# A 32-expert mixture kernel: third expert matrix read by row halves, both output halves accumulated together, first gate weights split before the overflow loop

## The chip, the cores and the metric

The program runs on one core of one Trainium2 chip. The metric is the device time of one execution in microseconds (us); lower is better. Three runs of the kernel before gave 2838.57, 2838.99 and 2841.83 us, a median of 2838.99. The profile is of another execution, of 2839.78 us.

Engines are named as in the profile: PE is the matrix engine (PEld its weight loads), DVE the vector engine, ACT the scalar engine, POOL GpSimd, SP the engine that issues most transfers. L932 means line 932 of the kernel before.

## The reference

A sequence of 1024 tokens of width 1024 goes through a mixer block, a mixture of experts, a gated addition, and two hybrid layers. The change lies in the experts and in the gate. Cut to what matters, the computation there is:

```python
# hier_moe: every token goes to 2 of 32 experts; per expert e, x: its rows
y = (silu(x @ w1[e]) * (x @ w3[e])) @ w2[e]     # w1, w3: 1024x512, w2: 512x1024, fp32
h = h + weighted_sum_of_the_two_y
# gate
h = h + rms_norm(p @ w_ple, g_ple) * sigmoid(rms_norm(h, g_plg) @ w_plg)   # w_plg: 1024x1024
```

All of it is fp32. The kernel keeps that precision by splitting each fp32 operand into a high and a low part and by adding three products: high by high, high by low weights, low by high weights.

## The kernel before

**An expert.** `moe()` (L1019) loops over 32 experts; `expert()` (L917) is a generator that does one. A gathered tile of 128 tokens (`xg`) is transposed on PE (L942), copied high by ACT (`exh`, L924) and low by DVE (`exl`, L926). The six weight pieces of an expert are 1 MB each (128 partitions by 2048 values): w1.0, w1.1, w3.0, w3.1 are row halves of w1 and w3; w2.0 and w2.1 are column halves of w2, which means 2 KB in one run of memory. I write e.w1.0 for such a piece of expert e. w1 goes into one PSUM bank, w3 into another, each with 24 matmuls of 128x512 (two halves of four 128-row blocks, three matmuls a block, L932 to L934). ACT takes the silu (`esg`, L959, two instructions), DVE multiplies (`ehd`, L960, two instructions), PE transposes four times (L965), ACT and DVE split the result (`ehh`, `ehl`). Then w2: for one column half after the other, 12 matmuls into a PSUM bank of its own and an evacuation by ACT (`ey`, L974); at the end POOL scatters the 128 rows to memory (`y_d`, L975). 72 matmuls of 128x512 and 12 transposes make an expert.

**Splitting weights.** A landed piece is split in four blocks of 128x512: ACT writes the high part (L115), DVE subtracts it from the raw data to get the low part (L116). The order of pieces is fixed by `seq`: e.w1.1, e.w3.1, (e+1).w1.0, (e+1).w3.0, e.w2.0, e.w2.1. Every third split goes to a single buffer `mhi`/`mlo`: these are e.w1.1 and (e+1).w3.0, in turn. The other four go to the two `whi`/`wlo` buffers in turn: e.w3.1 and e.w2.0 use one of them, (e+1).w1.0 and e.w2.1 the other. A split can only overwrite a buffer when the matmuls of the piece that was in it are done. Raw data lands in seven buffers that are used in a circle; SP issues the next load when the low part of the piece in a buffer is done.

**Order.** Each engine runs its instructions in the order of one list. That order is not the order of the Python code: a scheduler builds it, with its own estimate of when operands are ready. So one expert's w2 is mixed with the next expert's w1 and w3, and a change of a few lines can reorder the whole stage. Experts 4 to 11 also carry a tile of another product, `ple` (L699 to L708).

**Overflow and gate.** After the experts comes a loop for tokens that did not fit (`overflow()`, L982), which has no rounds with these inputs; its branch is a point in each engine's list that instructions are not moved across. Then `plg()` (L1110) reads the scattered rows back (`res`, `cy`, L1131 and L1133), adds them up (L1148, L1152), transposes (L241), and multiplies with w_plg in `wide()` (L162). `wide` takes the tiles in groups of four; a group goes through the first half of the weight's rows, then the second. The weight halves are loaded (L124) and split with a scale: four ACT instructions (L141) and four DVE instructions (L142) each. `wide` also serves the output projections, where `prep` makes the left operand of a tile.

Of the kernel before, what the change touches and what calls it, by code (L numbers as in the profile page):

```python
# [10 lines left out]
AF = mybir.ActivationFunctionType  # L11
# [7 lines left out]
NT = SEQ // 128  # L19
# [27 lines left out]
class Kernel:  # L47
# [113 lines left out]

    def wide(self, a, src, evac, group=4, prep=None, g=None):  # L162

        nc = self.nc
        w = [None, None]
        for t0 in range(0, NT, group):
            ps = [self.mm_ps() for _ in range(group)]
            for hf in range(2):  # L170
                if t0 == 0:
                    w[hf] = self.load_w(src[hf * 512:hf * 512 + 512], 4, 512, g=None if g is None else g[:, hf * 4:hf * 4 + 4])
                wh, wl = w[hf]
                for j in range(group):
                    tt = t0 + j
                    if prep and hf == 0:
                        prep(tt)
                    ah, al = a[tt // 4]
                    sl = slice(tt % 4 * 128, tt % 4 * 128 + 128)
                    for k in range(4):  # L180
                        f, l, ka = hf + k == 0, hf + k == 4, hf * 4 + k
                        nc.tensor.matmul(ps[j], ah[:, ka, sl], wh[:, k], start=f, stop=False)  # L182
                        nc.tensor.matmul(ps[j], ah[:, ka, sl], wl[:, k], start=False, stop=False)  # L183
                        nc.tensor.matmul(ps[j], al[:, ka, sl], wh[:, k], start=False, stop=l)  # L184
                    if hf:
                        evac(ps[j], tt)
# [730 lines left out]
    def expert(self, wp, xg, w1, w3, w2, sidx, native, after=None):  # L917


        nc = self.nc  # L920
        dt = F32 if native else F32R
# [45 lines left out]
        yield  # L967
        y = wp.tile([128, D], F32, name="ey", bufs=1)
        for c in range(2):
            ww = w2(c)  # L970
            q = self.mm_ps()
            for k in range(4):
                mm(q, (hh, hl), k, ww[:, k] if native else (ww[0][:, k], ww[1][:, k]), k == 0, k == 3)
            nc.scalar.activation(y[:, c * 512:c * 512 + 512], q, AF.Copy)  # L974
        yield nc.gpsimd.indirect_dma_start(  # L975
# [8 lines left out]
    def overflow(self):  # L984
# [9 lines left out]
        with self.banks(tp=3, mm=5), self.pool(name="ov", bufs=1) as wp:  # L994
            with tc.For_i(0, n, 1) as b:
# [8 lines left out]
                def w(name, rows):  # L1004
                    def f(c):
                        t = wp.tile([128, 4, 512], F32, name="ow")
                        cs = slice(c * 512, c * 512 + 512)
                        src = I[name][0, bass.ds(e, 1)]
                        src = src[:, cs] if rows else src[:, :, cs]
                        nc.sync.dma_start(t, src.rearrange("o (k p) n -> p (o k) n", p=128))  # L1010
                        return t
                    return f

                list(self.expert(wp, xg, w("w1", True), w("w3", True), w("w2", False), ix[:, 1:2], True))
        pre = nc.scalar.activation(self.done, self.done, AF.Copy)
# [3 lines left out]
    def moe(self, pgp):  # L1019
# [9 lines left out]
        with self.pool(name="mraw", bufs=1) as rw, ExitStack() as xs:  # L1029
# [6 lines left out]
            def fetch(key):  # L1036
# [4 lines left out]
                raw = b[0].tile([128, 2048], F32, name="mraw", tag=b[1]) if b else self.w_raw()  # L1041
                cs = slice(c * 512, c * 512 + 512)
                raws[key] = self.load_raw(raw, I[nm][0, e][:, cs] if nm == "w2" else I[nm][0, e][cs], 4, 512, dma=MOE_DMA)

# [64 lines left out]
    def plg(self, res, ple, norm):  # L1109
# [7 lines left out]
        with self.pool(name="pgn", bufs=1, side="right") as np_:  # L1117
# [6 lines left out]
            for tt, h in enumerate(hs):  # L1124
                nc.sync.dma_start(h, self.h1_d[tt * 128:tt * 128 + 128])
            pre = self.overflow()

# [31 lines left out]
        with ph, self.pool(name="ln", bufs=1, side="right") as ln, self.pool(name="pgc", bufs=1) as cp:  # L1159
# [4 lines left out]
            for c in range(2):  # L1164
# [12 lines left out]

                self.wide(ga, I["w_plg"][0][:, cs], evac, g=g)
            self.begin(0, lambda: cp.tile([128, 512], F32, name="psg", bufs=2)[:, :256])
# [452 lines left out]
```

## Time and profile before

| what | value |
|---|---|
| median of three runs | 2838.99 us |
| profiled execution | 2839.78 us, span 2838.0 us |
| mean granted PE clock | 0.981 of full speed |
| expert stage | 817 to 1440 us |
| PE busy over the span | 2667.1 us, 94% |
| DVE busy | 2089.5 us, 74% |
| ACT busy | 1763.0 us, 62% |
| memory traffic by DMA | 512.19 MB |

The span is the profiled execution from its first to its last instruction; 1.8 us of the execution lie outside it. A busy PE is no sign of a PE at its limit, because the ends of matmuls are modelled; so the distance between two starts is read, not the duration of one. In the answers a row gives the start in us, the duration (of a group of several, from the first start to the last end), the engine, the line, the operation, and the tiles as output<-inputs; in brackets stands how long the engine was idle before and what released it. The time of the stage can be read from POOL's scatters, one for each expert.

### The profile page before, as it was taken

The numbers are of one execution on the slowest core, as the hardware profiler recorded it, in microseconds if no ns is written. First come the engines' busy times: TensorE is split into PE (matmuls) and PEld (weight loads), VectorE is DVE, ScalarE is ACT, GpSimd is POOL, SyncE is SP. The second block draws the span as 40 slices with busy tenths as digits, with TensorE's granted clock in tenths as the row PEclk, the third lists the DMA queues.
The fourth block names the chain that finished last, engine by engine and source line by source line (L and its number), as shares of the span: only waits on it lengthen the run. The fifth ranks groups of instructions, "written<-read, shape, count | busy, mean of one in ns | idle before, by whom it ended". The sixth has DMA issues, their size and how long they took to land.

```text
span 2838.0 us, 46020 instructions
## 1 busy us (share of the span) xinstructions
PE 2667.1 (94%) x16247; PEld 2345.2 (83%) x16247; DVE 2089.5 (74%) x4266; ACT 1763.0 (62%) x3828; POOL 659.5 (23%) x688
## 2 busy tenths in 40 slices
PE   7999989899989999999979899999999999999988
PEld 7998968798768777877768788899878889999866
DVE  6778679885489888999966478899355479898254
ACT  4444467784348878888866367788343378787242
POOL 0344041360001102111014102650124103630132
PEclk9999989999989999999989899999999999999999
DMA  7765532244469989999962332332563433332561
GB/s 234 252 215 171 147 106 68 52 85 150 164 233 345 320 312 354 367 362 366 366 250 90 116 115 89 100 97 69 206 218 104 132 112 99 90 97 85 213 193 75
DMA packets 382701, 512.19 MB, mean 180 GB/s; under 512 B 95973, under 2 KB 220925, under 8 KB 381957
## 3 DMA queue, kind: packets, MB, share of 16 engines
q1 hardware_dynamic: 368068, 479.85, 51.2%
q0 software_dynamic: 14400, 29.38, 3.1%
q8 instruction: 129, 2.11, 0.3%
q14 instruction: 104, 0.84, 0.1%
HBM read 425.19 MB, written 101.97 MB: 186 GB/s over the span
## 4 chain that ended last, share of the span: by engine, by line
PE 25%; DVE 12%; ACT 5%; DMA 4%; issue 3%; POOL 1%; SPq 0%; DVEq 0%; ACTq 0%; POOLq 0%
PE mm L1278 3%; PE mm L1279 3%; PE mm L1280 3%; DVE sw L1452 3%; PE mm L184 2%; PE mm L183 2%; PE mm L182 2%; DMA sqk<-sk_d 2%; PE mm L158 2%; PE mm L160 2%; PE mm L159 2%; DVE sw L1451 1%; DVE sal L1471 1%; DVE sw L1457 1%; PE tp L1467 1%
## 5 line engine op out<-in xcount | busy, mean ns | idle before, releaser
L158 PE MATMUL mm<-whi,acth 128*128 128x256 f32 x1792 | 517.9, 289 | 11.3 <-DVE hn L325 3.4
L160 PE MATMUL mm<-whi,actl 128*128 128x256 f32 x1792 | 514.4, 287 | 0.2 <-DVE rsx L102 0.2
L159 PE MATMUL mm<-wlo,acth 128*128 128x256 f32 x1792 | 512.3, 286 | 0.0
L158 PEld LDWEIGHTS mm<-whi,acth 128*128 128x128 f32 x1792 | 345.1, 193 | 19.9 <-ACT rx L1319 4.8
L116 DVE TENSOR_TENSOR wlo<-mraw,whi 128x512 fp32r<-128x512 f32 x508 | 315.9, 682 | 48.1 <-ACT whi L115 47.8
L160 PEld LDWEIGHTS mm<-whi,actl 128*128 128x128 f32 x1792 | 344.5, 192 | 3.2 <-issue 0.7
L159 PEld LDWEIGHTS mm<-wlo,acth 128*128 128x128 f32 x1792 | 344.8, 192 | 2.6 <-issue 0.5
L115 ACT ACTIVATE whi<-mraw 128x512 fp32r<-128x512 f32 x508 | 276.0, 628 | 13.8 <-PE mm L934 8.6
L116 DVE TENSOR_TENSOR wlo<-wraw,whi 128x2048 fp32r<-128x2048 f32 (+1 forms) x60 | 132.9, 2219 | 126.0 <-ACT whi L115 123.9
L184 PE MATMUL mm<-whi,actl 128*128 128x512 f32 x512 | 202.0, 395 | 5.0 <-DVE actl L116 5.0
L182 PE MATMUL mm<-whi,acth 128*128 128x512 f32 x512 | 200.8, 397 | 4.7 <-ACT acth L115 4.7
L183 PE MATMUL mm<-wlo,acth 128*128 128x512 f32 x512 | 200.9, 393 | 1.4 <-DVE wlo L116 1.4
L1278 PE MATMUL mm<-acth,whi 128*128 128x512 f32 x512 | 201.4, 393 | 0.0
L1280 PE MATMUL mm<-acth,wlo 128*128 128x512 f32 x512 | 200.9, 392 | 0.0
L1279 PE MATMUL mm<-actl,whi 128*128 128x512 f32 x512 | 200.8, 392 | 0.0
L115 ACT ACTIVATE whi<-wraw 128x2048 fp32r<-128x2048 f32 (+1 forms) x60 | 109.4, 1827 | 97.9 <-PE mm L184 49.8
L116 DVE TENSOR_TENSOR mlo<-mraw,mhi 128x512 fp32r<-128x512 f32 x256 | 160.1, 680 | 2.9 <-ACT mhi L115 1.6
L1322 POOL TENSOR_TENSOR cN<-rx,rcos 128x256 f32<-128x256 f32 x64 | 58.6, 915 | 411.5 <-ACT rx L1319 407.8
L1458 ACT ACTIVATE sw<-sw 128x128 f32<-128x128 f32 (+2 forms) x192 | 100.1, 526 | 76.8 <-DVE sw L1457 75.6
L115 ACT ACTIVATE mhi<-mraw 128x512 fp32r<-128x512 f32 x256 | 140.6, 631 | 2.9 <-PE mm L934 2.9
L1451 DVE SCALAR_TENSOR_TENSOR sw<-z,sw 128x128 f32<-128x128 f32 (+1 forms) x192 | 103.8, 546 | 33.0 <-ACT sw L1450 32.4
L975 POOL DMA_INDIRECT y_d<-ey,sidx x32 | 38.9, 1216 | 372.2 <-ACT ey L974 365.0
(379 smaller groups left out, 7249.0 us busy)
## 6 DMA issues: line engine op xcount, KB each, us to landing
mraw<-in_w_dram SPq DMA_DIRECT2D x191, 1024.0 KB, 9.4
wraw<-in_w_in_dram SPq DMA_DIRECT2D x88, 512.0 KB, 5.0
mw<-in_w_ada_dram SPq DMA_DIRECT2D x32, 768.0 KB, 6.6
wraw<-in_w_out_dram SPq DMA_DIRECT2D x24, 512.0 KB, 5.2
q_d<-qo SPq DMA_DIRECT2D x32, 256.0 KB, 3.2
q<-q_d POOLq DMA_DIRECT2D x32, 256.0 KB, 3.0
h_d<-res SPq DMA_DIRECT2D x16, 512.0 KB, 2.9
sqk<-sq_d SPq DMA_DIRECT2D x32, 256.0 KB, 4.0
```

What stands on the lines that cost most here:

```text
L115: nc.scalar.activation(hi, raw, AF.Copy)
L116: nc.vector.tensor_sub(lo, raw, hi.bitcast(F32))
L158: nc.tensor.matmul(ps[:, :n], ah[:, k, sl], wh[:, k, :n], start=k == 0, stop=False)
L159: nc.tensor.matmul(ps[:, :n], ah[:, k, sl], wl[:, k, :n], start=False, stop=False)
L160: nc.tensor.matmul(ps[:, :n], al[:, k, sl], wh[:, k, :n], start=False, stop=k == kt - 1)
L182: nc.tensor.matmul(ps[j], ah[:, ka, sl], wh[:, k], start=f, stop=False)
L183: nc.tensor.matmul(ps[j], ah[:, ka, sl], wl[:, k], start=False, stop=False)
L184: nc.tensor.matmul(ps[j], al[:, ka, sl], wh[:, k], start=False, stop=l)
L1278: nc.tensor.matmul(ps, wh[:, k, cs], hh[:, k], start=k == 0, stop=False)
L1279: nc.tensor.matmul(ps, wh[:, k, cs], hl[:, k], start=False, stop=False)
L1280: nc.tensor.matmul(ps, wl[:, k, cs], hh[:, k], start=False, stop=k == 7)
L1451: nc.vector.scalar_tensor_tensor(a, z, 0.0, a, op0=OP.max, op1=OP.add)
```

## The change

1. w2 is read by row halves: w2.0 is rows 0 to 255 and w2.1 rows 256 to 511, each of 1024 columns, which means 4 KB in one run. A split block is now one 128-row block of one column half. Both column halves accumulate at once, in two PSUM banks that are open from w2.0's first to w2.1's last block, and both `ey` evacuations come after them. The overflow loop does the same.
2. `plg` loads and splits the first row half of w_plg for the first column half (`first`) before the overflow loop is entered, and hands it to `wide`.
3. `wide` calls `prep` for the second group of tiles during the second weight half of the first group.

The number of instructions of each kind stays.

```diff
--- before.py
+++ after.py
@@ -159,22 +159,25 @@
             nc.tensor.matmul(ps[:, :n], ah[:, k, sl], wl[:, k, :n], start=False, stop=False)
             nc.tensor.matmul(ps[:, :n], al[:, k, sl], wh[:, k, :n], start=False, stop=k == kt - 1)
 
-    def wide(self, a, src, evac, group=4, prep=None, g=None):
+    def wide(self, a, src, evac, group=4, prep=None, g=None, first=None):
+
 
 
 
         nc = self.nc
-        w = [None, None]
+        w = [first, None]
         for t0 in range(0, NT, group):
             ps = [self.mm_ps() for _ in range(group)]
             for hf in range(2):
-                if t0 == 0:
+                if w[hf] is None:
                     w[hf] = self.load_w(src[hf * 512:hf * 512 + 512], 4, 512, g=None if g is None else g[:, hf * 4:hf * 4 + 4])
                 wh, wl = w[hf]
                 for j in range(group):
                     tt = t0 + j
-                    if prep and hf == 0:
+                    if prep and hf == 0 and t0 == 0:
                         prep(tt)
+                    elif prep and hf and t0 + group < NT:
+                        prep(tt + group)
                     ah, al = a[tt // 4]
                     sl = slice(tt % 4 * 128, tt % 4 * 128 + 128)
                     for k in range(4):
@@ -917,6 +920,7 @@
     def expert(self, wp, xg, w1, w3, w2, sidx, native, after=None):
 
 
+
         nc = self.nc
         dt = F32 if native else F32R
 
@@ -966,12 +970,15 @@
         put(hh.rearrange("p a t -> p (a t)"), hl.rearrange("p a t -> p (a t)"), p)
         yield
         y = wp.tile([128, D], F32, name="ey", bufs=1)
+        qs = [self.mm_ps() for _ in range(2)]
         for c in range(2):
             ww = w2(c)
-            q = self.mm_ps()
-            for k in range(4):
-                mm(q, (hh, hl), k, ww[:, k] if native else (ww[0][:, k], ww[1][:, k]), k == 0, k == 3)
-            nc.scalar.activation(y[:, c * 512:c * 512 + 512], q, AF.Copy)
+            for k in range(2):
+                for n in range(2):
+                    b = k * 2 + n
+                    mm(qs[n], (hh, hl), c * 2 + k, ww[:, b] if native else (ww[0][:, b], ww[1][:, b]), c + k == 0, c + k == 2)
+        for n in range(2):
+            nc.scalar.activation(y[:, n * 512:n * 512 + 512], qs[n], AF.Copy)
         yield nc.gpsimd.indirect_dma_start(
             out=self.y_d[:, :], out_offset=bass.IndirectOffsetOnAxis(ap=sidx, axis=0), in_=y, in_offset=None,
             bounds_check=2 * SEQ - 1, oob_is_err=False)
@@ -1004,14 +1011,13 @@
                 def w(name, rows):
                     def f(c):
                         t = wp.tile([128, 4, 512], F32, name="ow")
-                        cs = slice(c * 512, c * 512 + 512)
-                        src = I[name][0, bass.ds(e, 1)]
-                        src = src[:, cs] if rows else src[:, :, cs]
-                        nc.sync.dma_start(t, src.rearrange("o (k p) n -> p (o k) n", p=128))
+                        src = I[name][0, bass.ds(e, 1)][:, c * rows:c * rows + rows]
+                        nc.sync.dma_start(t.rearrange("p a b -> p (a b)").rearrange("p (k n) -> p k n", k=rows // 128),
+                                          src.rearrange("o (k p) n -> p (o k) n", p=128))
                         return t
                     return f
 
-                list(self.expert(wp, xg, w("w1", True), w("w3", True), w("w2", False), ix[:, 1:2], True))
+                list(self.expert(wp, xg, w("w1", 512), w("w3", 512), w("w2", 256), ix[:, 1:2], True))
         pre = nc.scalar.activation(self.done, self.done, AF.Copy)
         with tc.issue_after(pre.ins):
             return nc.scalar.preload_act_table_set("natural_log_exp_and_others")
@@ -1039,8 +1045,9 @@
                 n[0] += 1
                 b = order[j] if j < NF else bufs[(j - NF) % len(bufs)]
                 raw = b[0].tile([128, 2048], F32, name="mraw", tag=b[1]) if b else self.w_raw()
-                cs = slice(c * 512, c * 512 + 512)
-                raws[key] = self.load_raw(raw, I[nm][0, e][:, cs] if nm == "w2" else I[nm][0, e][cs], 4, 512, dma=MOE_DMA)
+                r = 256 if nm == "w2" else 512
+                self.load_raw(raw, I[nm][0, e][c * r:c * r + r], r // 128, 262144 // r, dma=MOE_DMA)
+                raws[key] = raw.rearrange("p (k n) -> p k n", n=512)
 
             def split(key, pieces=PIECES):
                 n[1] += 1
@@ -1123,6 +1130,7 @@
             hs = [hw[0][:, :D], hw[0][:, D:], hw[1][:, :D]]
             for tt, h in enumerate(hs):
                 nc.sync.dma_start(h, self.h1_d[tt * 128:tt * 128 + 128])
+            first = self.split_w(self.load_raw(self.w_raw(), I["w_plg"][0][:512, :512], 4, 512), self.w_hl(), g=g[:, :4])
             pre = self.overflow()
 
             def rows(tt):
@@ -1175,7 +1183,7 @@
                     if c:
                         done(res, tt)
 
-                self.wide(ga, I["w_plg"][0][:, cs], evac, g=g)
+                self.wide(ga, I["w_plg"][0][:, cs], evac, g=g, first=None if c else first)
             self.begin(0, lambda: cp.tile([128, 512], F32, name="psg", bufs=2)[:, :256])
 
 
```

The lists of the engines differ from the start of the expert stage on; ahead of it they are the same. Three places follow. Numbers behind a name tell buffers apart; lines of the changed kernel are 4 to 8 higher.

First PE, at the end of w1.1 of an expert late in the stage (before, expert 27). mm_15390 is that expert's w1 bank, mm_15391 its w3 bank, exh and exl its input:

```order
5762 L934 MATMUL mm_15390<-mhi_15517,exl_15312 128x512
5763 L932 MATMUL mm_15390<-mhi_15517,exh_15311 128x512
5764 L933 MATMUL mm_15390<-mlo_15518,exh_15311 128x512
5765 L934 MATMUL mm_15390<-mhi_15517,exl_15312 128x512
5766 L932 MATMUL mm_15391<-whi_15541,exh_15311 128x512
5767 L933 MATMUL mm_15391<-wlo_15542,exh_15311 128x512
5768 L934 MATMUL mm_15391<-whi_15541,exl_15312 128x512
```

The same place after; whi_15445 and whi_15469 are w2.0 and w2.1 of expert 26, ehh and ehl that expert's input, mm_15442 the bank of its second column half:

```order
5754 L937 MATMUL mm_15390<-mlo_15518,exh_15311 128x512
5755 L938 MATMUL mm_15390<-mhi_15517,exl_15312 128x512
5756 L936 MATMUL mm_15442<-whi_15445,ehh_15381 128x512
5757 L937 MATMUL mm_15442<-wlo_15446,ehh_15381 128x512
5758 L938 MATMUL mm_15442<-whi_15445,ehl_15382 128x512
5759 L936 MATMUL mm_15442<-whi_15445,ehh_15381 128x512
5760 L937 MATMUL mm_15442<-wlo_15446,ehh_15381 128x512
5761 L938 MATMUL mm_15442<-whi_15445,ehl_15382 128x512
5762 L936 MATMUL mm_15442<-whi_15469,ehh_15381 128x512
```

Before, w3.1 follows w1.1 at once. After, twelve matmuls come between, the second column half of the earlier expert's w2 (six with w2.0, six with w2.1); the first column half's twelve stand ahead of w1.1. This recurs every 76 rows, seven times, from row 5452 to row 5908, and in nearly this form once ahead of these and once behind.

Second ACT, one period of the late stage, from one silu to the next, before:

```order
971 L959 ACTIVATE esg<-mm 128x256 x2
972 L115 ACTIVATE whi<-mraw 128x512 x4
973 L974 ACTIVATE ey<-mm 128x512 x2
974 L924 ACTIVATE exh<-tp 128x512 x2
975 L924 ACTIVATE ehh<-tp 128x512
976 L115 ACTIVATE mhi<-mraw 128x512 x4
977 L115 ACTIVATE whi<-mraw 128x512 x8
978 L115 ACTIVATE mhi<-mraw 128x512 x4
979 L115 ACTIVATE whi<-mraw 128x512 x4
```

and after:

```order
975 L963 ACTIVATE esg<-mm 128x256 x2
976 L115 ACTIVATE whi<-mraw 128x512 x8
977 L115 ACTIVATE mhi<-mraw 128x512 x4
978 L928 ACTIVATE exh<-tp 128x512 x2
979 L928 ACTIVATE ehh<-tp 128x512
980 L115 ACTIVATE whi<-mraw 128x512 x8
981 L115 ACTIVATE mhi<-mraw 128x512 x4
982 L981 ACTIVATE ey<-mm 128x512 x2
```

The four copies of w3.1, which closed a period before the silu, now open the next one behind it; the copies of w3.0 moved ahead of exh, and ey to the period's end.

Third DVE, around the overflow loop's end, before:

```order
1689 L995 UNCONDITIONAL_BRANCH
1690 L142 SCALAR_TENSOR_TENSOR wlo<-wraw,gplg,whi 128x512
1691 L1148 SCALAR_TENSOR_TENSOR res<-res,wk,h_16385 128x1024
1692 L142 SCALAR_TENSOR_TENSOR wlo<-wraw,gplg,whi 128x512 x3
1693 L1152 SCALAR_TENSOR_TENSOR res<-cy,wk,res 128x1024
1694 L1148 SCALAR_TENSOR_TENSOR res<-res,wk,h_16385 128x1024
```

and after:

```order
1685 L1002 UNCONDITIONAL_BRANCH
1686 L1156 SCALAR_TENSOR_TENSOR res<-res,wk,h_16385 128x1024
1687 L1160 SCALAR_TENSOR_TENSOR res<-cy,wk,res 128x1024
1688 L1156 SCALAR_TENSOR_TENSOR res<-res,wk,h_16385 128x1024
1689 L1160 SCALAR_TENSOR_TENSOR res<-cy,wk,res 128x1024
```

The four L142 instructions now stand ahead of the loop, and the two sums of a tile follow each other. On SP the load of the second row half of w_plg moves ahead of the loop as well.

## Rows read from the trace of the kernel before

**Rows 1.** Windows: us, busy us (instructions) by engine, granted PE clock, DMA share, GB/s.
```profile
core 0: us, PE busy (x) PEld busy (x) DVE busy (x) ACT busy (x) POOL busy (x), PEclk, DMA share, GB/s
850.00:1000.00 150.00, 149.16 (x680) 116.93 (x679) 135.69 (x242) 124.05 (x252) 16.30 (x14) 1.00 0.93 331
1000.00:1100.00 100.00, 96.43 (x427) 74.63 (x426) 81.54 (x140) 77.28 (x160) 11.25 (x10) 1.00 0.92 321
...
1300.00:1400.00 100.00, 95.37 (x450) 77.76 (x449) 90.88 (x156) 83.95 (x167) 10.06 (x10) 1.00 1.01 367
...
1450.00:1460.00 10.00, 6.60 (x23) 5.26 (x24) 8.95 (x11) 5.66 (x10) 0.00 (x0) 0.50 1.02 402
```

**Rows 2.** Timeline of POOL: scatters of experts 18 and 29.
```profile
1208.33 1.01 POOL L975 DMA_INDIRECT y_d<-ey,sidx  x1 [16.41 <-ACT ey L974]
...
1414.82 0.97 POOL L975 DMA_INDIRECT y_d<-ey,sidx  x1 [17.78 <-ACT ey L974]
```

**Rows 3.** Waits, 1196 to 1422 us: engine line <- releaser: us in total, times, longest.
```profile
ACT esg L959 <- PE mm L934: 30.1, 12, 2.5
...
PE mm L933 <- DVE mlo L116: 8.5, 11, 0.8
```

**Rows 4.** Timeline of PE in one period of the late stage.
```profile
1320.40 0.38 PE L965 MATMUL tp<-ident,ehd 128*128 128x128 f32 x2
...
1321.63 0.48 PE L933 MATMUL mm<-wlo,exh 128*128 128x512 f32 x1
...
1323.57 0.39 PE L932 MATMUL mm<-mhi,exh 128*128 128x512 f32 x1
1324.73 0.50 PE L933 MATMUL mm<-mlo,exh 128*128 128x512 f32 x1 [0.77 <-DVE mlo L116]
...
1327.39 0.39 PE L932 MATMUL mm<-whi,ehh 128*128 128x512 f32 x1
...
1332.60 0.39 PE L934 MATMUL mm<-whi,ehl 128*128 128x512 f32 x1
```

**Rows 5.** Timeline of ACT in the same period.
```profile
1316.97 0.66 ACT L959 ACTIVATE esg<-mm 128x256 f32<-128x256 f32 x2 [2.53 <-PE mm L934]
...
1322.71 2.20 ACT L115 ACTIVATE mhi<-mraw 128x512 fp32r<-128x512 f32 x4
1324.78 4.28 ACT L115 ACTIVATE whi<-mraw 128x512 fp32r<-128x512 f32 x8
...
1335.75 0.66 ACT L959 ACTIVATE esg<-mm 128x256 f32<-128x256 f32 x2 [2.52 <-PE mm L934]
```

**Rows 6.** Timeline of DVE in the same period.
```profile
1319.69 0.75 DVE L960 TENSOR_TENSOR ehd<-mm,esg 128x256 f32<-128x256 f32 x2 [0.82 <-PE mm L934]
1320.36 1.92 DVE L116 TENSOR_TENSOR wlo<-mraw,whi 128x512 fp32r<-128x512 f32 x3
...
1326.41 4.89 DVE L116 TENSOR_TENSOR wlo<-mraw,whi 128x512 fp32r<-128x512 f32 x8
1331.22 2.48 DVE L116 TENSOR_TENSOR mlo<-mraw,mhi 128x512 fp32r<-128x512 f32 x4
```

**Rows 7.** Tile mraw (raw weights), 1300 to 1337 us: its last line.
```profile
DMA to landing us min/median/max: 9.1/9.5/9.7
```

**Rows 8.** Waits of SP's queue, 850 to 1440 us.
```profile
SPq L124 <- DVE wlo L116: 335.5, 111, 14.9
```

**Rows 9.** Timeline of all engines, from the last scatter to the gate's first transpose.
```profile
1440.58 0.97 POOL L975 DMA_INDIRECT y_d<-ey,sidx  x1 [7.24 <-DVEq L995]
...
1446.29 2.56 ACT L141 ACTIVATE whi<-wraw,gplg 128x512 fp32r<-128x512 f32 x4
...
1448.32 1.28 DVE L1148 SCALAR_TENSOR_TENSOR res<-res,wk,h 128x1024 f32<-128x1024 f32 x1 [0.53 <-DMA res<-y_d]
1449.52 2.07 DVE L142 SCALAR_TENSOR_TENSOR wlo<-wraw,gplg,whi 128x512 fp32r<-128x512 f32 x3
1451.51 1.27 DVE L1152 SCALAR_TENSOR_TENSOR res<-cy,wk,res 128x1024 f32<-128x1024 f32 x1
...
1452.84 0.48 PE L241 MATMUL tp<-ident,res 128*128 128x128 f32 x1 [13.17 <-DVE res L1152]
```

## The prediction

> **What bounds the kernel now.** I read the windows first, to see which engine is full in which stage, then the waits of the stage that the change touches, then one period of it on PE, ACT and DVE side by side, then the transfers, and last the join between experts and gate.
>
> Between 850 and 1000 us PE is busy 149.16 of 150 us, between 1000 and 1100 us 96.43 of 100, later 95.37 of 100 [rows 1]. DVE follows with 90.88 of 100 in the late stretch; the granted clock is 1.00 there. So PE is the limit, with DVE close behind it. An expert's time is the distance between scatters: eleven periods lie between 1208.33 and 1414.82 [rows 2], 18.77 us each.
>
> Where they go: from 1327.39 to 1332.60 there are 23 steps of a 128x512 matmul [rows 4], 0.2265 us each. An expert has 72, which is 16.31 us. The twelve transposes take from 1320.40 to 1321.63, 1.23 us. One matmul on a low part in `mlo` starts at 1324.73, 1.16 us behind the one ahead of it, so 0.93 us are lost there. The sum is 18.47; the remaining 0.30 is spread over slightly longer steps behind that wait. This wait is the one that PE has in every period: 8.5 us in 11 times [rows 3]. ACT waits for PE 2.5 us before each silu in the same rows; it has room.
>
> The other prices: an ACT copy of 128x512 follows the one ahead by (1324.78 - 1322.71)/4 = 0.52 us and lasts 0.64 [rows 5]. A DVE subtraction follows by (1331.22 - 1326.41)/8 = 0.601 us and lasts 0.68; the two `ehd` take 0.67 together [rows 6]. A silu starts 0.20 us after the last matmul of w1.1 is through: the last w2 matmul starts at 1332.60, thirteen steps later it is 1335.55, and the silu starts at 1335.75 [rows 4, 5].
>
> Transfers: a raw piece lands 9.5 us after its issue [rows 7]. Seven buffers go round at six pieces in 18.77 us, so one comes back after 21.9 us; with some 2.5 us for its four subtractions a landed piece waits about 10 us to be split. SP's waits say the same: its queue waits for DVE to free a buffer, 111 times [rows 8], and no engine's wait in the stage names a raw load.
>
> **4 KB instead of 2 KB in one run.** The transfers have 10 us of slack in a period, so I cost this at nothing; what hides it is that slack. The bound on the other side: the stretch from 1300 to 1400 us moves 367 GB/s at a DMA share of 1.01, one behind the experts 402 [rows 1]. If transfers set the period, it could shrink by the ratio, 1.6 us, and no further than PE's own 17.54. A page speaks against a gain here: the Trainium skill, DMA: Bandwidth & Descriptors, Specifications, gives about 358 GB/s as a core's share of memory and 512 B as the shortest transfer at full rate. By the first the six pieces of 6.29 MB would take 17.6 us at best, by the second longer runs than 2 KB would buy nothing. The trace does not bear out the first as a ceiling, since 402 GB/s stand in its rows; that runs over 512 B differ in nothing no row shows.
>
> **Both column halves at once, as the lists have it.** This is the large term. Instruction counts stay, so PE's 16.31 + 1.23 us stay; what changes is who waits. In the late stage (seven periods exactly, two more nearly) PE's list puts the twelve matmuls of the second column half behind the next expert's w1.1, six on w2.0 and six on w2.1, and ACT's copies of w3.1 go behind the silu. w3.1 goes into the buffer that w2.0 held, which is now read until after w1.1. I walk one period, T = 0 at the silu:
>
> PE was through with w1.1 at -0.20. The six matmuls on w2.0 end at 6 x 0.2265 - 0.20 = 1.16. ACT can overwrite the buffer 0.20 later, at 1.36, and DVE's first subtraction starts when that copy is done, at about 2.05. DVE had finished the low parts of w1.1 before T = 0 and so stood idle for some 3 us across the period's start. From 2.05 on it has in its list w3.1, w1.0 and w3.0 (12 subtractions), two `exl`, one `ehl`, w2.0 and w2.1 (8): 23 x 0.601 = 13.82, and the two `ehd` with 0.67. That is unbroken, because ACT does its 12 copies by 1.36 + 12 x 0.52 = 7.6 and stays ahead of it. DVE comes to the low part of w1.1 at 16.54; the first block is there at 17.22. PE has had its other work done by then and waits; from 17.25 it needs eleven more steps, 2.49, and is through at 19.74. The next silu starts at 19.94.
>
> So the period is 19.9 instead of 18.77, +1.17. The sum for before fell 0.30 short of what was measured; if the same is missing here it is +1.47. I take 1.3. The bounds are wide: with no wait at all the period would be 17.54 + 0.2, a gain of 1.0; with the full shortfall it is 1.5 dearer. I stand near the upper end because the chain holds only three engines in a fixed list with prices from neighbouring rows. Nine such periods: **+11.7 us**.
>
> The period ahead of these runs the first column half of w2.0 and w2.1 first, so that PE takes every second block that DVE makes: a block costs PE 0.68 and DVE two subtractions, 1.20. Four blocks lose up to 2.1, of which the 0.93 of before falls away: **+1.1**. Two periods still earlier copy w3.0 ahead of `exh`, so the wait on `mlo` shrinks; I take half of it: **-0.9** for both. For the experts before these, with `ple` and without, PE has idle time of 0.84 us in 150 and of 3.57 us in 100 [rows 1], so there is at most some 4 us to gain; a loss of 0.5 us in each of a dozen reordered periods bounds the other side at +6. I take 0.
>
> Both `ey` now follow the last matmul of the stage, where only one did: one more ACT step ahead of the last scatter, **+0.5**.
>
> **First gate weights ahead of the loop.** Before, DVE runs three L142 instructions between the two sums of the first tile, L1148 at 1448.32 and L1152 at 1451.51, and PE's first transpose starts behind that, at 1452.84 after 13.17 us idle [rows 9]. Now L1152 can follow at 1449.52, where the L142 instructions start: **-2.0**. It can be 0 if the second row block (`cy`) has not landed by then; it is asked for right behind the first one, so I take the whole. The eight moved instructions (ACT's 2.56 us, DVE's four) run in the last expert's shadow, where ACT has few copies left; if they pushed the last `ey`, they would cost at most those 2.56. The load of the second weight half moves to before the loop on SP; it is done before the scattered rows are asked for, so it costs nothing, and if it were late it would push them by its own 2.6 us at the most (1.05 MB at 402 GB/s). After the idle time PE runs at half the clock (0.50 between 1450 and 1460 [rows 1]); that stays, only earlier.
>
> **`prep` earlier in `wide`.** In the two layers the transposes of the second group stand some three matmuls earlier at one place each. Two places at 3 x 0.2265 bound it to 1.4 either way: 0.
>
> The sum: 11.7 + 1.1 - 0.9 + 0.5 - 2.0 = **+10.4 us**. On the profiled execution's 2839.78 that is 2850.2; this execution lies 0.79 above the median of the runs, so for the median I say 2849.4. A measurement of this kernel can tell about 0.2%, 5.7 us.
>
> **Rivals.**
> *PE stays the bound (faster).* If DVE does not stand idle at a period's start, because the copies of w3.1 find a free buffer, the second column half's twelve matmuls give DVE 2.7 us of time and the wait on `mlo` goes. For it: PE had only 0.93 us to lose. Against it: w3.1 and w2.0 share one of two buffers. Nine periods at -1.0, -0.9, +0.5 and the join's -2.0: 2838.99 - 11.4 = 2827.6.
> *Transfers were the limit (faster).* Then 4 KB runs take 1.2 us (to PE's 17.54) out of each of about twelve periods: with the join 2838.99 - 14.8 - 1.5 = 2822.7. Against it: 10 us of slack [rows 7, 8].
> *The lists' order costs little (same).* With 0.2 us a period instead of 1.3 the whole is +1.8 + 0.2 - 1.5, 2839.5. It would take a DVE chain that is shorter by a twentieth than I reckon.
> *`ey` holds the banks (slower still).* Five PSUM banks serve the stage; two are now held by a w2 until ACT evacuates both, behind its copies of w1.1. In my walk these end at about 16.3, ahead of PE's need at 19.74. If ACT came 3.4 us later than I reckon, PE would wait for the two `ey`; it decides from there, and their two steps, 1.04, would be added to nine periods: 2849.4 + 9.4 = 2858.8.
>
> **How the numbers follow.** The forecast has 0.55, with a range of its own from 2842 (0.5 us a period) to 2856 (2 us). PE as the bound 0.14, transfers 0.07, little cost 0.16, `ey` 0.08. Slower by over 0.2% (above 2844.7) are the forecast but for a small part, and `ey`: 0.61. Within: 0.18. Faster: 0.21. The range runs from 2829, which leaves out the transfers and a part of the first rival, to 2861.
>
> **What would show it.** In the late stage the scatters should be 19.9 to 20.1 us apart; DVE should wait for ACT's copies some 3 us in each period, and PE for low parts some 2.4 us instead of 0.8. Raw loads should still land in about 10 us with nobody waiting for them. PE's first transpose of the gate should follow the last scatter by about 10.3 us instead of 12.3. If the scatters stay 18.8 apart or closer, the step "DVE idle until w3.1's buffer is free" is wrong; if an engine waits on a raw load, the slack is.

## The result and the profile after

The changed kernel takes 2865.14 us (median of four runs, 2862.50 to 2868.73), against 2838.78 us for the kernel before on the same chips. The ratio is 1.0088, with a 95% interval of 1.0074 to 1.0102: 26 us slower. I had forecast 10.4 us slower, with a range up to 2861. The sign was right; more than half of the loss was not foreseen.

The profiled execution took 2866.79 us with a span of 2865.0 us, 27.0 us longer than the span before. The span can be cut at events that both traces have. The table is worked out from their starts.

| stretch | before | after | difference | forecast |
|---|---|---|---|---|
| start to first scatter | 843.6 | 842.9 | -0.7 | 0 |
| first to last scatter (experts) | 597.0 | 615.6 | +18.6 | +12.4 |
| last scatter to ACT's `done` (overflow loop passed) | 4.2 | 7.3 | +3.1 | 0 |
| `done` to the gate's first transpose | 8.1 | 6.2 | -1.9 | -2.0 |
| gate's first to last transpose | 40.5 | 39.5 | -1.0 | 0 |
| to the last transpose ahead of layer 1 | 733.2 | 736.0 | +2.8 | 0 |
| layer 1, to the last matmul of L1278 | 473.8 | 481.5 | +7.7 | 0 |
| to the end of the span | 137.6 | 136.1 | -1.5 | 0 |

One thing must be known to read this and the tables below. Profiles of kernels with the same list up to the first scatter differ by up to 6.5 us ahead of it (839.1 to 845.7 us in the changed kernel and three with its list there). So stages are compared by their own length, and whole kernels by their medians.

**The late expert stage.** A window of the changed kernel, with the columns of [rows 1]; it answers to the window from 1300 to 1400 there:

```profile
1300.00:1400.00 100.00, 95.31 (x420) 71.20 (x418) 84.47 (x146) 78.65 (x155) 16.07 (x9) 1.00 0.97 341
```

The share in which PE is busy has not moved (95.37 before), but it starts 420 instructions in 100 us where it started 450. A busy share would have shown nothing; the count does. DMA now moves 341 GB/s instead of 367, since it is asked for less. The scatters, as in [rows 2], on POOL:

```profile
1300.17 2.05 POOL L982 DMA_INDIRECT y_d<-ey,sidx  x1 [6.96 <-ACT ey L981]
...
1380.60 2.05 POOL L982 DMA_INDIRECT y_d<-ey,sidx  x1 [6.96 <-ACT ey L981]
```

There are four periods between them, 20.11 us each instead of 18.77. The forecast was 19.9 to 20.1. Now the waits of 100 us there (us in total, times, longest), five periods:

```profile
DVE wlo L116 <- ACT whi L115: 16.6, 5, 4.1
...
ACT whi L115 <- PE mm L938: 3.6, 5, 0.8
PE mm L937 <- DVE wlo L116: 2.4, 10, 0.3
PE mm L937 <- DVE mlo L116: 2.4, 5, 0.5
```

DVE stands idle 3.3 us in each period for ACT's copies, where before the same wait took 0.84 (4.2 us in five periods); ACT waits for PE ahead of one copy in each period. PE's waits for low parts come to 1.0 us a period in this view, where I had expected 2.4. By the distances between starts PE loses more: 2.5 us over its plain steps between 1322.30 and 1342.42, and 1.2 in the same period before. Most of it lies at three blocks of w2 and at w1.1. The chain is plain in one period on ACT:

```profile
1322.50 0.66 ACT L963 ACTIVATE esg<-mm 128x256 f32<-128x256 f32 x2 [2.57 <-PE mm L938]
1323.86 4.28 ACT L115 ACTIVATE whi<-mraw 128x512 fp32r<-128x512 f32 x8 [0.70 <-PE mm L938]
...
1342.62 0.66 ACT L963 ACTIVATE esg<-mm 128x256 f32<-128x256 f32 x2 [2.55 <-PE mm L938]
```

and on DVE:

```profile
1318.93 2.51 DVE L116 TENSOR_TENSOR mlo<-mraw,mhi 128x512 fp32r<-128x512 f32 x4
1324.52 4.31 DVE L116 TENSOR_TENSOR wlo<-mraw,whi 128x512 fp32r<-128x512 f32 x7 [3.09 <-ACT whi L115]
...
1339.02 2.50 DVE L116 TENSOR_TENSOR mlo<-mraw,mhi 128x512 fp32r<-128x512 f32 x4
```

From the silu at 1322.50, ACT's copies of w3.1 begin 1.36 us later (forecast 1.36), DVE 2.02 later (2.05), the low part of w1.1 16.52 later (16.54), and the next silu 20.12 later (19.94). No engine's wait in these 100 us names a raw load. The last line of the tile mraw from 1300 to 1337 us, as in [rows 7]:

```profile
DMA to landing us min/median/max: 7.4/7.8/8.2
```

**The end of the stage.** The silus draw apart here. ACT, silus and the copies ahead of them:

```profile
1402.93 0.66 ACT L963 ACTIVATE esg<-mm 128x256 f32<-128x256 f32 x2 [2.57 <-PE mm L938]
...
1423.98 4.28 ACT L115 ACTIVATE whi<-mraw 128x512 fp32r<-128x512 f32 x8 [4.67 <-PE mm L938]
1428.17 0.63 ACT L963 ACTIVATE esg<-mm 128x256 f32<-128x256 f32 x2
```

Eight copies stand ahead of the silu and not behind it, and they wait for PE, because w2's second column half still holds the buffer. The period is 25.24 us, 6.5 longer than the same one before (18.77). But PE does not lose these 6.5 us: it goes on with 22 matmuls of the next pieces, from 1425.59 to 1430.35, without a gap. PE's own delay is read by places in PE's order: the start of the thousandth instruction, say, in one trace against that in the other, less their difference at the first scatter. PE is 1.02 us late at the place that it reached at 1204.4 before, 2.40 at 1241.9, 4.20 at 1260.6, 14.33 at 1392.1, 15.68 at 1410.9, 16.61 at 1430.2, and 18.35 at the last matmul. So the two late silus cost PE 1.35 and 0.93 us, no more than the periods ahead of them. The last 1.74 come behind them: PE is idle 0.79 us ahead of the last transposes and 1.67 us ahead of the last w2, and then runs at half clock:

```profile
1450.00:1453.00 3.00, 2.82 (x7) 2.24 (x8) 1.02 (x2) 0.13 (x1) 1.27 (x1) 0.50 0.93 371
```

Twelve matmuls take 4.24 us there (1450.18 to 1454.42), 1.5 more than at full clock; before, the granted clock was 1.00 at this place.

**Between experts and gate.** Timeline of all engines, as in [rows 9]:

```profile
1457.09 1.05 ACT L981 ACTIVATE ey<-mm 128x512 f32<-128x512 f32 x2
...
1457.45 0.75 DVE L142 SCALAR_TENSOR_TENSOR wlo<-wraw,gplg,whi 128x512 fp32r<-128x512 f32 x1
1458.22 1.85 SPq L124 DMA_DIRECT2D wraw<-in_w_plg_dram  x2
1458.42 0.97 POOL L982 DMA_INDIRECT y_d<-ey,sidx  x1 [7.15 <-DVEq L1002]
1465.62 0.34 SPq L1139 DMA_DIRECT2D res<-y_d  x1
1465.70 0.20 ACT L1021 ACTIVATE done<-done 128x1 f32<-128x1 f32 x1 [7.55 <-DMA wraw<-in_w_plg_dram]
...
1469.23 1.29 DVE L1156 SCALAR_TENSOR_TENSOR res<-res,wk,h 128x1024 f32<-128x1024 f32 x1 [11.03 <-DMA res<-y_d]
1470.57 1.28 DVE L1160 SCALAR_TENSOR_TENSOR res<-cy,wk,res 128x1024 f32<-128x1024 f32 x1
...
1471.91 0.48 PE L244 MATMUL tp<-ident,res 128*128 128x128 f32 x1 [14.61 <-DVE res L1160]
```

The two sums of the tile follow each other at last, and that part gained its 1.9 us. But the load of the second weight half (two transfers of 0.5 MB) is issued at 1458.22, 0.2 us ahead of the last scatter, and the scattered rows are asked for 7.20 us after the scatter instead of 4.03. The row of `done` names what it waited for: the load, not the scatter. Waits of SP's queue at the loop's end (L1002), 1457 to 1466 us:

```profile
SPq L1002 <- DMA wraw<-in_w_plg_dram: 1.6, 1, 1.6
...
SPq L1002 <- DMA y_d<-ey,sidx: 0.8, 1, 0.8
```

and the landing of the last scatter, after and before:

```profile
DMA to landing us min/median/max: 4.8/4.8/4.8
DMA to landing us min/median/max: 3.2/3.2/3.2
```

At the end of the loop SP and ACT wait for 24 semaphores, those of the scatter and of the load among them. The scatter lands 1.6 us later than before, and the load itself 2.0 us behind it, 6.8 us after the scatter's issue.

**Layer 1.** Two lines of each trace give its bounds: the transposes of `xn` (the last one is ahead of layer 1) and the matmuls L1278 or, after, L1286 (the last one is near its end); both show count, durations in ns, first and last start. Before:

```profile
L241 PE MATMUL tp<-ident,xn x192: 270/273/476, 8.9 to 2226.6; 128*128 128x128 f32 x192
L1278 PE MATMUL mm<-acth,whi x512: 387/389/485, 1598.5 to 2700.4; 128*128 128x512 f32 x171
```

After:

```profile
L244 PE MATMUL tp<-ident,xn x192: 270/273/476, 8.9 to 2247.4; 128*128 128x128 f32 x192
L1286 PE MATMUL mm<-acth,whi x512: 387/389/628, 1615.7 to 2728.9; 128*128 128x512 f32 x171
```

Layer 1 takes 2728.9 - 2247.4 = 481.5 us, where it took 473.8. Of its code only the place of `prep` was changed.

### The profile page after: what moved, and what is told of

Its sections match the earlier page's. It is cut to its first block, busy times and chain, and to the rows that moved or that the text cites. A ratio compares the mean times of both kernels' runs of the same rounds, so it can differ in the third digit from the quotient of the medians.

```text
span 2865.0 us, 46024 instructions
## 1 busy us (share of the span) xinstructions
PE 2684.1 (94%) x16247; PEld 2346.3 (82%) x16247; DVE 2090.4 (73%) x4266; ACT 1761.7 (61%) x3828; POOL 708.8 (25%) x688
## 5 line engine op out<-in xcount | busy, mean ns | idle before, releaser
L1286 PE MATMUL mm<-acth,whi 128*128 128x512 f32 x512 | 202.1, 395 | 0.0
L115 ACT ACTIVATE mhi<-mraw 128x512 fp32r<-128x512 f32 x256 | 140.6, 628 | 12.4 <-PE mm L938 12.4
L987 POOL DMA_INDIRECT xg<-xf_d,gidx x32 | 47.9, 1498 | 351.5 <-PE tp L946 170.0
L982 POOL DMA_INDIRECT y_d<-ey,sidx x32 | 75.2, 2350 | 241.1 <-ACT ey L981 234.0
```

The source lines that it names most:

```text
L115: nc.scalar.activation(hi, raw, AF.Copy)
L1286: nc.tensor.matmul(ps, wh[:, k, cs], hh[:, k], start=k == 0, stop=False)
```

## The experiments

Eleven kernels were run. They tell apart three losses: in the experts, at the join between experts and gate, in layer 1.

**Only the change to w2.** The kernel before with part 1 of the change.

> The kernel before with the change to w2 alone (row halves, both column halves at once); the gate's weights and prep as before. Theory: the expert stage takes all of its 17.6 us from this part, because the second column half's matmuls stand behind the next w1.1 and hold the buffer that w3.1 needs; late periods 20.1 us apart, and the layers, whose lists are those of before, add nothing: 2855 to 2858 us. Rival, that the w2 part also slows what follows (as the changed kernel is 26 us slower in all): 2865 us.

2853.76 us, ratio 1.0055 (1.0038 to 1.0072) to a kernel before that ran at 2840.49. The stage from first to last scatter takes 615.4 us, as in the changed kernel (615.6). Layer 1 takes 473.6, as before. The late periods:

```profile
1316.63 2.11 POOL L978 DMA_INDIRECT y_d<-ey,sidx  x1 [6.91 <-ACT ey L977]
...
1397.02 2.07 POOL L978 DMA_INDIRECT y_d<-ey,sidx  x1 [18.02 <-ACT ey L977]
```

Four periods of 20.10 us. So all of the experts' loss comes from the w2 part, and it does not spread behind them. The median rose by 13 us and not by the 17 expected; the profiled run lost 18.4 in the stage and was 4.5 us shorter ahead of the first scatter.

**Only the gate's first weights.** The kernel before with part 2 of the change.

> The kernel before with the gate's first weights split ahead of the overflow loop, and nothing else. Its expert stage has the list of before; its second layer has the list of the changed kernel. Theory: the second half's load, now ahead of the loop, delays the landing of the last scatter by 3 us and the gate starts 1 to 2 us later instead of 2 earlier; the second layer's list then costs some 6 us: 2845 to 2848 us. Rival, that the losses outside the expert stage only follow from the experts' part: 2836 to 2838 us.

2847.10 us, ratio 1.0025 (1.0016 to 1.0035). The end of the stage on SP, ACT and PE:

```profile
1443.08 2.25 SPq L124 DMA_DIRECT2D wraw<-in_w_plg_dram  x2
...
1450.43 0.20 ACT L1015 ACTIVATE done<-done 128x1 f32<-128x1 f32 x1 [7.43 <-DMA wraw<-in_w_plg_dram]
...
1458.05 1.97 PE L241 MATMUL tp<-ident,res 128*128 128x128 f32 x8 [15.89 <-DVE res L1153]
```

The last scatter was issued at 1443.28; `done` comes 7.15 us later, 4.20 before. Layer 1 takes 482.2 us. So part 2 alone brings both late losses, without the new w2: the rival falls. The theory that the load delays the scatter's landing by 3 us holds in part: it lands after 4.4 us instead of 3.2, and the rest of the wait is for the load itself, as the row of `done` says.

**The second half's load held back.** As the one ahead, but with that load behind the first two pairs of row reads on SP:

```diff
-                    w[hf] = self.load_w(...)
+                    with self.tc.issue_after(held.ins) if held else nullcontext():
+                        w[hf] = self.load_w(...)
...
             ry = [rows(tt) for tt in range(2)]
+            self.cyd = self.wdma
...
-                self.wide(ga, I["w_plg"][0][:, cs], evac, g=g, first=None if c else first)
+                self.wide(ga, I["w_plg"][0][:, cs], evac, g=g, first=None if c else first, held=None if c else self.cyd)
```

> The kernel before with the gate's first weights split ahead of the loop, and the load of the second half held behind the first two pairs of row reads, as it stood before; the second layer's list is that of before again. Theory: the last scatter lands as before, the gate's first transpose comes 1.5 to 2 us earlier, the layers add nothing: 2836 to 2838 us. Rival, that the split itself is what delays the last scatter (its copies stand ahead of the last ey on ACT): 2841 us.

2838.84 us, ratio 0.9999 (0.9989 to 1.0008).

```profile
1439.19 0.98 POOL L976 DMA_INDIRECT y_d<-ey,sidx  x1 [7.48 <-ACTq L996]
...
1443.38 0.20 ACT L1016 ACTIVATE done<-done 128x1 f32<-128x1 f32 x1 [4.46 <-DMA y_d<-ey,sidx]
...
1450.10 1.12 PE L242 MATMUL tp<-ident,res 128*128 128x128 f32 x4 [12.10 <-DMA cy<-y_d]
```

`done` follows the scatter by 4.19 us and the first transpose follows `done` by 6.72 (8.06 before): the split ahead of the loop is worth 1.3 us here. Layer 1 is back at 474.0. A gain of that size cannot be told from none in the median.

**The changed kernel with the same load held back.**

> The changed kernel with one thing moved: the load of the gate's second weight half is held behind the first two pairs of row reads on SP. With that the second layer's list is that of the kernel before (four matmuls of the first layer's output projection apart). Theory: the last scatter lands 3 us earlier, the second layer gives back some 7 us, the expert stage keeps its 17.6: 2853 to 2857 us. Rival, that the layers lose time for another reason than their list: 2861 us or more.

2857.04 us, ratio 1.0067 (1.0051 to 1.0082).

```profile
L245 PE MATMUL tp<-ident,xn x192: 270/273/476, 8.7 to 2246.6; 128*128 128x128 f32 x192
L1288 PE MATMUL mm<-acth,whi x512: 387/389/485, 1619.0 to 2720.7; 128*128 128x512 f32 x171
```

Layer 1 takes 474.1 us, `done` follows the scatter by 4.5, the stage keeps its 615.7. One moved load takes away both late losses. `prep` stays as in the changed kernel here, and from layer 1 on PE's order is again that of before, so `prep` is not what changed it.

**2 KB runs with the new matmuls.** The changed kernel; each row half of w2 is read by two transfers of one column half:

```diff
-                self.load_raw(raw, I[nm][0, e][c * r:c * r + r], r // 128, 262144 // r, dma=MOE_DMA)
+                if nm == "w2":
+                    for n2 in range(2):
+                        nc.sync.dma_start(raw.rearrange("p (k n) -> p k n", n=1024)[:, :, n2 * 512:n2 * 512 + 512],
+                                          I[nm][0, e][c * r:c * r + r, n2 * 512:n2 * 512 + 512].rearrange("(k p) n -> p k n", p=128))
```

> The changed kernel with each 1 MB row half of w2 read by two transfers of one column half each, so that a run in memory is 2 KB again; data, splits and matmuls as in the changed kernel. Its expert list is that of the changed kernel late in the stage; its second layer has the list of before. Theory: no engine waits for a raw load, so the run length moves nothing: late periods 20.1 us, stage as in the changed kernel, and in all 2856 to 2860 us, less than the changed kernel only by the second layer's list. Rival, that 4 KB runs gain something that the list's order hides: late periods longer than 20.3 us.

2849.96 us, ratio 1.0037 (1.0023 to 1.0051), 6 us below the range that I expected.

```profile
1318.84 3.10 POOL L982 DMA_INDIRECT y_d<-ey,sidx  x1 [4.72 <-ACT ey L981]
...
1399.28 3.08 POOL L982 DMA_INDIRECT y_d<-ey,sidx  x1 [17.00 <-ACT ey L981]
```

Late periods are 20.11 us, the same as with 4 KB, so the run length moves nothing there. The list is not quite that of the changed kernel (its stage takes 612.5 us, 3 less), so the whole says nothing of the run length. Layer 1 takes 474.3 us with the list of before, though the load is not held.

**Six PSUM banks.** The changed kernel; in the expert stage six banks for products and two for transposes:

```diff
-                with self.banks(tp=3, mm=5), ...
+                with self.banks(tp=2, mm=6), ...
```

> The changed kernel with six PSUM banks for products and two for transposes in the expert stage, in place of five and three. Theory: the second column half stands behind w1.1 only because no sixth bank is free; with one, w2's matmuls are together again in the list, w3.1's copy has its buffer early, late periods are 18.8 us or less, and the second layer has the list of before: 2838 to 2843 us. Rival, that 4 KB runs or two open banks cost time by themselves: late periods stay near 20 us, 2855 us or more.

2834.76 us, ratio 0.9982 (0.9971 to 0.9993).

```profile
1301.55 1.00 POOL L982 DMA_INDIRECT y_d<-ey,sidx  x1 [14.24 <-ACT ey L981]
...
1374.69 1.00 POOL L982 DMA_INDIRECT y_d<-ey,sidx  x1 [14.24 <-ACT ey L981]
```

Late periods of 18.29 us, from 20.11. Layer 1, with the list of before, takes 474.1. In this kernel's list w2's 24 matmuls are together again ahead of w1.1. An expert's two w2 banks, held until ACT evacuates them, and two banks each for this expert and the next make six; with five, half of w2 has to wait. The rival falls: neither 4 KB nor two open banks cost time. It also lost something at the stage's end:

```profile
1435.55 1.09 ACT L981 ACTIVATE ey<-mm 128x512 f32<-128x512 f32 x2
1442.89 1.09 ACT L981 ACTIVATE ey<-mm 128x512 f32<-128x512 f32 x2 [6.25 <-DMA y_d<-ey,sidx]
```

The last matmul starts at 1435.15; the last scatter comes 9.1 us later, 1.3 before. There is one `ey` buffer, and the last expert's `ey` waits for the scatter ahead of it to land.

**Six banks, old w2.** The kernel before with the same banks.

> The kernel before with six PSUM banks for products and two for transposes in the expert stage. Theory: the gain of six banks over the kernel before, seen with the new w2, comes from the banks and the list they give, not from w2: late periods fall from 18.78 to 18.3 us here too. Rival, that it takes both halves at once to get there: late periods 18.8 us. The second layer has a third list, of unknown cost, so the stage is compared and not the whole.

2846.32 us, ratio 1.0025 (1.0013 to 1.0036).

```profile
1296.19 1.00 POOL L975 DMA_INDIRECT y_d<-ey,sidx  x1 [14.44 <-ACT ey L974]
...
1370.17 1.00 POOL L975 DMA_INDIRECT y_d<-ey,sidx  x1 [14.43 <-ACT ey L974]
```

Late periods of 18.50 us, between the expected 18.3 and the rival's 18.8. With the old w2 the sixth bank gains 0.27 us a period; with six banks the new w2 gains another 0.2. The stage takes 591.0 us, 6.0 less than before. The whole is slower because layer 1 got a third list, with 483.7 us, and the part ahead of it takes 740.1 instead of 733.2.

**Six banks, new w2, the gate's split behind the loop.**

> The new w2 with six banks, and the gate's first weights split behind the loop as before. Theory: the six-bank run lost 7 us between its last matmul and its last scatter, because the copies of the gate's weights stood ahead of the last two pairs of ey on ACT; without them the last scatter follows the last matmul by 1.3 us and the whole is 2828 to 2832 us, if the second layer's list (a third one) costs no more than 2 us. Rival: the scatter is late by itself (9 us behind the last matmul), 2835 us.

2849.95 us, ratio 1.0047 (1.0030 to 1.0065). Both parts of the expectation failed. The last scatter is still 6.4 us behind the last matmul, though the gate's copies are gone; so the single `ey` buffer does it by itself, now that both halves' `ey` stand at the end. And the third list of layer 1 costs 485.7 us.

**Six banks, two `ey` buffers, split ahead, load held.**

> The new w2 with six banks and two ey buffers, the gate's first weights split ahead of the loop, the second half's load held behind the first row reads. Theory: with a second buffer the last expert's ey need not wait for the scatter ahead of it to land, so the split costs at most the 2.6 us of its copies, and the gate starts 8 us behind the last scatter's landing less 2: 2827 to 2831 us, about 1 us better than without the split. Rival: the copies push the last scatter by as much as they save, no difference to the run without the split.

2852.54 us, ratio 1.0053 (1.0037 to 1.0070), where I expected 2827 to 2831. The last scatter follows the last matmul by 1.5 us, so the second buffer cures that. But this list has late periods of 18.89 us (the next run shows why), and the third list of layer 1, 485.0 us. The gain at the join is lost among these.

**Six banks and two `ey` buffers, old w2.**

> The kernel before (old w2) with six and two banks and two ey buffers, nothing else; the second layer keeps the list of before. Theory: late periods 18.5 us as with six banks and one buffer, the last pair of ey does not wait for a scatter to land: 2832 to 2835 us. Rival, that the other place of the transposes in this list (behind w3.1) costs the gain: 2839 us.

2852.20 us, ratio 1.0051 (1.0037 to 1.0065): the rival, and worse. Waits of five late periods:

```profile
DVE ehd L960 <- ACT whi L115: 9.3, 5, 1.9
...
PE tp L965 <- DVE ehd L960: 2.9, 5, 0.6
```

With the second buffer the transposes stand directly behind w3.1 in PE's list, and PE waits 0.6 us there for `ehd`: 19.1 us a period, from 18.5. The run ahead of this one has the same wait, 2.9 us in five periods. Layer 1 (475.4) had the list of before.

**Six banks, old w2, split ahead, load held behind three pairs.** A combination whose two layers have the list of before.

> The kernel before (old w2) with six PSUM banks for products and two for transposes, the gate's first weights split ahead of the loop, and the second half's load held behind the third pair of row reads; both layers keep the list of before. Theory: the expert stage gains the 5.2 us that six banks gave with the old w2, the join 1 us: 2832 to 2835 us. Rival, that the join loses as in the six-bank run with the new w2: 2839 us.

2827.20 us, ratio 0.9962 (0.9950 to 0.9974): 10.6 us faster than the kernel before and the best of all here.

```profile
1300.76 1.00 POOL L976 DMA_INDIRECT y_d<-ey,sidx  x1 [14.44 <-ACT ey L975]
...
1374.63 1.00 POOL L976 DMA_INDIRECT y_d<-ey,sidx  x1 [14.43 <-ACT ey L975]
```

Late periods of 18.47 us, the stage 591.3 (-5.7), the join 1.3 shorter, layer 1 473.8. Another 3.4 us, between gate and layer 1 (729.8 after 733.2), I had not expected. PE is at half clock for 20.5 us of that stretch, where it was for 27.3 before, which would be worth 3.4; but the kernel with the split and the held load alone has 20.5 us too and takes 734.1, so this is not shown to be the cause.

## Why the prediction was right in sign and too small

Three steps failed: the layers at nothing, the load that "costs nothing", and the experts' periods ahead of the steady ones.

**4 KB runs at nothing: right.** Late periods are 20.11 us with either run length, and no wait names a raw load. The weighing against the Trainium skill (DMA: Bandwidth & Descriptors, Specifications) stands as it was: its 512 B does not speak against a run length that does nothing, though a stage in which nobody waits for loads would not show a gain; and its 358 GB/s is passed by the 402 of [rows 1].

**The late period: right, with its mechanism.** The walk gave 19.94 and I took 1.3 us a period; 20.11 and 1.34 were measured. Nine periods cost PE 12.4 us (from 4.20 late to 16.61 late), where I had 11.7. Six banks undo it, and w2's matmuls are together again there: the second column half's place in the list, forced by the banks, is the cause. I had looked at the banks only as a rival about `ey` and did not ask why the list had split w2.

**The periods ahead of these: the step that failed in the experts.** I put the two still earlier at -0.9, because the wait on `mlo` would shrink. It is gone, but PE waits for the low parts of w2.0 instead, block by block, as I had priced it only for the period ahead of the nine. From 1232.89 to 1237.32 there are four such waits, 1.8 us between starts, for 0.93 at `mlo` before. These two periods cost 1.4, the one that I had at 1.1 cost 1.8, and the experts ahead, which I put at 0, 1.0.

**The end of the stage: too small.** I priced it by one more `ey`, 0.5 us. It is 2.0 from the end of the nine periods to the last scatter, 1.5 of it at half clock. The forecast for the experts was 12.4 and the loss 18.6; of the 6.2 between them 0.7 belong to the nine periods, 4.0 to those ahead and 1.5 to the end.

**The gate's weights: the gain was right, the cover was not.** Putting the sums one behind the other gave 1.9 us (forecast 2.0). "It is done before the scattered rows are asked for" was wrong. The split itself cannot run early, because its high part goes into a buffer that the last expert's w2 holds: ACT waits for PE and DVE finishes at 1458.20. Only then is the raw buffer free, and the load goes out 0.2 us ahead of the scatter. The loop's end waits for it, and the scatter lands later beside it. That cost 3.1 us; I had named 2.6 us as the price of a late load, and gave that case no weight. The first transpose follows the last scatter by 13.5 us, where I had 10.3.

**The layers at nothing: the largest step that failed.** I looked at the two places of `prep` and put the rest at zero. But the list of layer 1 differs: 1630 of the 3666 PE instructions from its start to the end stand in other places in the changed kernel, and nearly the same ones with part 2 alone. Eight kernels, the one before among them, have the list of before there and take 473.6 to 475.4 us. The two with the changed list take 7.7 and 8.4 more; a third list, which three six-bank kernels got, costs 10 to 12. The clock does not explain it: PE is at half clock for 3.4 us of layer 1 in the changed kernel, and for as long in the kernel with the split and the held load, at 474.0. Holding the load brings the list of before back, but it also comes with the load not held, in the 2 KB run and in the six-bank run of the changed kernel. So the load is not all that the list turns on; what else does was not tried. Part 3 (`prep`) moves four matmuls on PE and was not run alone; the changed kernel with the load held, which has it, takes 474.1 us in layer 1 and 733.4 ahead of it. The 2.8 us between gate and layer 1 stay open: the six-bank kernel with the new w2 has the same list there and takes 732.1 us, 3.9 less. The changed kernel has one more stretch of 3.4 us at half clock there, worth 1.7 us at most, and two kernels with the list of before behind the gate differ by as much (729.8 in the fastest, 734.7 with part 2 alone).

So the 26 us are 18 from w2's second half, 1 from the join and about 8 from a list of layer 1 that nobody asked for.

## What to carry to other kernels

Where a scheduler writes the lists, compare the lists of the whole program, not only of the code that was changed, and ask of every change how many accumulators are open at once: one bank too few turned a harmless reordering into 1.3 us an expert. Walk the rounds that lead into the steady ones, and the last, as well as the one that repeats; and measure a loss on the engine that is the limit, since a late step on another engine may cost it nothing. A prefetch is only early if its buffer is; find out what frees it, and what waits for it to land.

## What the runs showed of the hardware that I had not expected

A scatter on POOL's queue lands later beside a load on SP's: with 1 MB issued 0.2 us ahead of it, the last scatter landed 4.8, 4.4 and 4.5 us after its issue in three kernels; without it 3.2 to 3.7 us in the nine others whose traces tell (in one of them the load was issued 7.8 us ahead). The end of a loop without rounds still waited for that load to land: `done` followed the scatter by 7.28, 7.15 and 7.19 us with it, and by 4.2 to 4.7 without (ten kernels). Raw pieces landed in 7.8 us with 4 KB runs in the changed kernel and in 9.5 before, but the transfers were also asked for less often there; in the old w2's kernel with 19.1 us periods they landed in 8.3, and with 4 KB runs and 18.3 us periods in 9.3, so this does not show what a longer run is worth.
